# Cumulative decays from split fp32r parts, and rate products on both halves of the rows

## The chip, the cores and the metric

The kernel runs on one core of a Trainium2 chip. The metric is the device time of one execution in microseconds. Three executions of the kernel before took 2044.55 (median), 2040.88 and 2045.95 us. All data is fp32; nothing is computed on the host but the layout of the inputs.

## The reference

The reference is a stack of two transformer blocks on 256 latent and 256 context tokens with 1024 features: a hybrid block (an RWKV mixer beside differential attention), a state-space block, and a second model with three attention branches. The change lies in the RWKV mixer's preparation. Per direction d, with the projections `wd`, `ad`, `k` of the tokens:

```
wlog  = -softplus(-(w0[d] + tanh(wd) @ w_up[d])) - 0.5
decay = exp(-exp(wlog))
a     = sigmoid(a0[d] + ad @ a_up[d])          # the rate
kmod  = k * (1.0 + (a - 1.0) * k_a)
# scan:  s = s * w_t + (s @ -kk_t) b_t + v_t k_t ;  y_t = s @ r_t
```

The scan multiplies a state by a decay at each of 256 steps, forward and backward. The kernel works on chunks of 64 tokens instead of single steps, for which it needs the decays accumulated within each chunk. Since exp(wlog) is exp(-0.5) times sigmoid of `w0 + tanh(wd) @ w_up`, and sigmoid(x) is half of tanh(x/2) + 1, the accumulated log decay is a constant times a running sum of tanh(x/2) + 1 over the chunk's tokens.

## The kernel before, in words

The kernel is a sequence of stages. Each stage is written as Python generators ("streams") that yield a declared cost; `weave` takes the next step from the stream that is least far along. A planner then orders each engine's instructions in advance, by priority and by its own estimate of when operands are ready, and puts in the semaphores; at run time each engine goes through its list in order. Tiles come from pools with a fixed number of buffers per tag, and buffers of a tag are handed out in program order. A stage's pools reuse the memory of the stage before, so its first tiles wait until the last reader of the old ones is done.

The stage of the change is in `hybrid` (L672), between about 46 and 216 us. It has two streams:

- `dense` (L745): 17 projections of 512 columns (256 context, 256 latent tokens). Each is 24 fp32r matmuls (`projs`, L447): weights and activations are split into a rounded high part and a low part (`whi`, `wlo`, `hhi`, `hlo`), and three of the four products are kept. The first projection gives `wdad`: rows 0 to 63 are `wd`, rows 64 to 127 are `ad`. Then come k, r, v for the four pairs of heads p, the gate, and q, k, v of the first attention head.
- `preps` (L766): `rwkv_prep` for p = 0 to 3. It runs with a priority 1000 ahead of the dense stream.

`rwkv_prep(p)` (L1120) first makes the rate: for d = 0, 1 one fp32 product of 64 contraction rows and 512 columns (L1130), tanh (L1132), and `kmod` on VectorE (L1134, L1135). Then come the unit keys (L1145 to L1152), v reversed and transposed (L1159 to L1167) and the bonus (L1172 to L1177). Then, for each direction: `pw`, the product for the decay (L1182, four token blocks), tanh (L1185), plus one (L1186), and for each half s (context, latent) the running sums within chunks, as a product of `w` with a 128x256 matrix of zeros and ones, `tri0` or `tri1` (L1193): its first 128 columns give the inclusive sum, the others the exclusive one. Two exponentials (L1197, L1198) and four VectorE products (L1211 to L1214) give `ar` and `bk`; `bk` is transposed (L1218), copied to SBUF (L1220), and all three are stored to DRAM by GpSimd's DMA queue (`bkd`, `ard`, `btd`, L1221 to L1223). Products on PSUM bank tag `w` take their banks in program order, so the second half's L1193 stands behind the first half's L1218. The tag `mm` has two banks.

A full fp32 product appears in the trace as two matmul instructions, an fp32r product as one. fp32r rounds its operands; a matrix of zeros and ones is exact in it.

After the stage, `rwkv_units` (L930) reads the stored tiles back, beside `diff_attention` (L810) and the modulation products `adas` (L454, matmuls L473, loads `raw<-adaw`). Matmuls of these streams stand in TensorE's list from 186 us on, as far as their buffers allow; the tiles that they need in the pools `DF` and `U` open when the stage's pools `Q` and `X` are free. Weights are loaded by SyncE's queue into four buffers `raw` (L410), in program order.

Of the kernel before, what the change touches and what calls it, by code (L numbers as in the profile page):

```python
# [7 lines left out]
F32 = mybir.dt.float32  # L8
# [294 lines left out]
class Kern:  # L303
# [368 lines left out]
    def hybrid(self):  # L672
# [17 lines left out]
        nc.scalar.dma_start(wup, A['wup'])  # L690
        aup = self.tl(Q, [128, 2, 512], 'aup')
        nc.scalar.dma_start(aup[64:128], A['aup'])
        omm = self.tl(Q, [128, 14], 'omm')
# [11 lines left out]
        nc.vector.tensor_scalar(hrk, self.V('r_k'), 0.5, None, op0=MUL)  # L705
        self.load_consts(5, Q)

        def shifted(b, out):
# [19 lines left out]
        sig = self.sig = self.tl(R, [128, 512], 'sig')  # L728
        wdad = self.tl(Q, [128, 512], 'wdad')
        wt = self.tl(Q, [65, 512], 'wt')  # L730
        t4 = lambda n: [self.tl(Q, [128, 512], n, bufs=4) for _ in range(4)]
# [13 lines left out]
        def dense():  # L745
            yield from shifted(0, wdad)
            nc.scalar.activation(wt[0:64], wdad[0:64], AF.Tanh)
            nc.gpsimd.memset(wt[64:65], 1.0)
            for hf in range(2):
# [16 lines left out]
        def preps():  # L766
            for hf in range(2):
                yield from await_(main, lambda: (hf, 0) in ready)
                yield from unit_keys(hf)
                yield from await_(main, lambda: (hf, 2) in ready)  # L770
                for j in range(2):
                    p = 2 * hf + j
                    yield from self.rwkv_prep(p, ks[p], rr[p], vv[p], yk[hf][:, 8 * j:8 * j + 8], wdad, wt, wup, aup,
                                              ha0, hka, oka, hrk, Q, X)

# [343 lines left out]

    def rwkv_prep(self, p, k, r, v, yk, wdad, wt, wup, aup, ha0, hka, oka, hrk, Q, X):  # L1120

# [4 lines left out]
        nc.vector.tensor_scalar(kok, k, oka[:, p:p + 1], None, op0=MUL)  # L1126
        kms, ts = [], []
        for d in range(2):
            ps = self.PSt('w')
            nc.tensor.matmul(ps, aup[64:128, d, 128 * p:128 * p + 128], wdad[64:128], start=True, stop=True)  # L1130
            t = self.tl(X, [128, 512], 'x1', bufs=2)
            nc.scalar.activation(t, ps, AF.Tanh, scale=0.5, bias=ha0[:, d, p:p + 1])  # L1132
            km = self.tl(Q, [128, 512], 'km', bufs=2)
            nc.vector.tensor_tensor(km, t, k, MUL)  # L1134
            nc.vector.scalar_tensor_tensor(km, km, hka[:, p:p + 1], kok, op0=MUL, op1=ADD)  # L1135
            kms.append(km)
            ts.append(t)
            yield 1.5
# [40 lines left out]
        for d in range(2):  # L1179
            pw = self.PSt('w')  # L1180
            for tt in range(4):
                nc.tensor.matmul(pw[:, 128 * tt:128 * tt + 128], wt[:, 128 * tt:128 * tt + 128],  # L1182
                                 wup[:, d, 128 * p:128 * p + 128], start=True, stop=True)
            w = self.tl(Q, [128, 512], 'w', bufs=1)
            nc.scalar.activation(w, pw, AF.Tanh, scale=0.5)  # L1185
            nc.vector.tensor_scalar(w, w, 1.0, None, op0=ADD)  # L1186
            wh = w.rearrange("p (a b) -> p a b", a=4)
            yield 2.0
            for s in range(2):
                pg = self.PSt('w').rearrange("p (t k c) -> p t k c", t=2, k=2)  # L1190
                for dt in range(2):
                    for i, x in enumerate((wh,)):
                        nc.tensor.matmul(pg[:, dt], x[:, 2 * s + (dt if d == 0 else 1 - dt)], self.C(f'tri{d}'),  # L1193
                                         start=True, stop=True)
                eP = self.tl(X, [128, 2, 2, 128], 'eP', bufs=2)
# [1078 lines left out]
```

## Time and profile before

| | |
|---|---|
| median of three executions | 2044.55 us |
| profiled execution, its own time | 2040.4 us |
| its span | 2038.6 us |
| TensorE busy | 1938.1 us, 95% of the span |
| VectorE busy | 1446.8 us, 71% |
| ScalarE busy | 964.4 us, 47% |
| GpSimd busy | 149.9 us, 7% |
| mean granted TensorE clock | 0.978 of full speed |

Engines are named PE (TensorE matmul), PEld (its weight loads, which overlap), DVE (VectorE), ACT (ScalarE), POOL (GpSimd) and SP (SyncE). L1193 is line 1193 of the kernel. A row such as `168.70 1.13 PE L1193 MATMUL psw<-cst,w ... x4` is four instructions, the first starting at 168.70 us; output left of the arrow, operands right. A matmul's length in the timeline includes its way through the array (some 0.17 us here), so that neighbours overlap; the chain of waits shows what each added. In brackets stands idle time of the engine ahead of the row and what ended it. A granted clock of 1.00 is TensorE's level of 2.4 GHz, 0.50 that of 1.2 GHz.

### The profile page before, as it was taken

What the parts mean: (1) busy time and instruction counts of PE and PEld (TensorE: products, weight loads), DVE (VectorE), ACT (ScalarE), POOL (GpSimd) and SP (SyncE); (2) the same over time, 40 slices, a digit from 0 to 9 for tenths busy, and PEclk for the clock granted to TensorE, in tenths of its full rate; (3) what the DMA queues carried; (4) which work ended last, traced back from release to release, by engine and by line L of the source; (5) the groups of instructions that cost most, each with busy time, mean ns of one, the idle gap of its engine ahead of it and who ended that gap; (6) DMA issues with size and microseconds to landing.
All of it is one profiled execution on the core that took longest, in us unless ns stands there. A gap on an engine that the chain in (4) does not pass through costs nothing.

```text
span 2038.6 us, 37380 instructions
## 1 busy us (share of the span) xinstructions
PE 1938.1 (95%) x14898; PEld 1648.5 (81%) x14898; DVE 1446.8 (71%) x3044; ACT 964.4 (47%) x1770; POOL 149.9 (7%) x273
## 2 busy tenths in 40 slices
PE   6999799969899999998999999999999999999999
PEld 4776456747698899986778878899986888899999
DVE  4675596696699854437988887666678666667984
ACT  3454233322552434434566665566655445456663
POOL 0022401201031200000000003000000000000000
PEclk8999898989899999999999999999999999999999
DMA  7355843413287853322223325466644323345664
GB/s 274 125 175 203 251 155 120 143 42 124 81 271 243 289 169 93 94 88 71 92 64 86 101 73 158 147 186 185 180 148 153 125 93 115 113 147 173 191 190 150
DMA packets 87021, 299.82 MB, mean 147 GB/s; under 512 B 11213, under 2 KB 14685, under 8 KB 86846
## 3 DMA queue, kind: packets, MB, share of 16 engines
q1 hardware_dynamic: 62064, 221.29, 34.1%
q0 software_dynamic: 20736, 69.64, 10.5%
q10 hardware_dynamic: 4046, 6.49, 1.0%
q8 instruction: 117, 1.92, 0.4%
q14 instruction: 58, 0.48, 0.1%
HBM read 281.63 MB, written 18.90 MB: 147 GB/s over the span
## 4 chain that ended last, share of the span: by engine, by line
PE 79%; DVE 8%; DMA 5%; issue 5%; ACT 2%; POOL 1%; POOLq 0%; SPq 0%; DVEq 0%; ACTq 0%
PE psmm L447 23%; PE psmm L426 11%; PE psmm L429 11%; PE psmm L427 11%; DMA ar<-adat 2%; PE psmm L1635 2%; PE psy L1698 2%; PE psw L524 1%; PE psw L1703 1%; DVE wlo L419 1%; PE psa L429 1%; PE psa L426 1%; PE psa L427 1%; PE pso L2054 1%; PE psya L972 1%
## 5 line engine op out<-in xcount | busy, mean ns | idle before, releaser
L418 ACT ACTIVATE whi<-raw 128x1024 fp32r<-128x1024 f32 x374 | 394.4, 1055 | 482.1 <-PE psmm L427 242.2
L419 DVE TENSOR_TENSOR wlo<-raw,whi 128x1024 fp32r<-128x1024 f32 x374 | 453.5, 1213 | 59.4 <-ACT whi L418 39.1
L447 PE MATMUL psmm<-hhi,whi 128*128 128x256 f32 (+1 forms) x1040 | 337.4, 346 | 6.5 <-ACT whi L418 2.1
L447 PE MATMUL psmm<-hlo,whi 128*128 128x256 f32 (+1 forms) x1040 | 330.9, 339 | 2.1 <-DVE hlo L665 1.5
L426 PE MATMUL psmm<-hhi,whi 128*128 128x258 f32 (+1 forms) x944 | 231.1, 283 | 0.3 <-ACT whi L418 0.3
L427 PE MATMUL psmm<-hlo,whi 128*128 128x258 f32 (+1 forms) x944 | 230.8, 282 | 0.0
L447 PEld LDWEIGHTS psmm<-hhi,whi 128*128 128x128 f32 x1040 | 199.8, 192 | 38.1 <-issue 12.2
L447 PEld LDWEIGHTS psmm<-hlo,whi 128*128 128x128 f32 x1040 | 199.7, 192 | 28.7 <-DVE hlo L663 4.8
L447 PE MATMUL psmm<-hhi,wlo 128*128 128x256 f32 (+1 forms) x1040 | 213.5, 336 | 0.2 <-DVE wlo L419 0.2
L426 PEld LDWEIGHTS psmm<-hhi,whi 128*128 128x128 f32 x944 | 178.7, 189 | 2.7 <-issue 1.4
L427 PEld LDWEIGHTS psmm<-hlo,whi 128*128 128x128 f32 x944 | 179.2, 190 | 0.7 <-issue 0.6
L447 PEld LDWEIGHTS psmm<-hhi,wlo 128*128 128x128 f32 x1040 | 157.4, 189 | 25.1 <-issue 9.1
L426 PE MATMUL psmm<-hi,whi 128*128 128x512 f32 (+1 forms) x512 | 164.0, 340 | 5.3 <-ACT hi L668 5.3
L427 PE MATMUL psmm<-lo,whi 128*128 128x512 f32 (+1 forms) x512 | 161.8, 336 | 0.0
L429 PE MATMUL psmm<-hhi,wlo 128*128 128x258 f32 (+1 forms) x944 | 132.0, 282 | 0.0
L429 PEld LDWEIGHTS psmm<-hhi,wlo 128*128 128x128 f32 x944 | 121.0, 190 | 0.0
L426 PEld LDWEIGHTS psmm<-hi,whi 128*128 128x128 f32 x512 | 96.4, 189 | 19.1 <-ACT hi L668 7.0
L511 DVE SCALAR_TENSOR_TENSOR aj<-ar,cb 128x1024 f32<-128x1024 f32 x80 | 97.8, 1222 | 13.2 <-DMA ar<-adat 10.2
L427 PEld LDWEIGHTS psmm<-lo,whi 128*128 128x128 f32 x512 | 96.3, 189 | 10.3 <-DVE lo L669 0.5
L429 PE MATMUL psmm<-hi,wlo 128*128 128x512 f32 (+1 forms) x512 | 100.0, 338 | 0.0
L1370 ACT ACTIVATE r<-r,s 128x256 f32<-128x256 f32 x96 | 48.9, 510 | 87.8 <-DVE r L1369 87.5
L429 PEld LDWEIGHTS psmm<-hi,wlo 128*128 128x128 f32 x512 | 81.6, 190 | 10.4
(607 smaller groups left out, 3649.0 us busy)
## 6 DMA issues: line engine op xcount, KB each, us to landing
raw<-w SPq DMA_DIRECT2D x128, 512.0 KB, 4.1
ar<-adat POOLq DMA_DIRECT2D x56, 512.0 KB, 4.9
raw<-win SPq DMA_DIRECT2D x55, 512.0 KB, 3.5
raw<-ssdin SPq DMA_DIRECT2D x49, 512.0 KB, 3.6
raw<-hyin SPq DMA_DIRECT2D x26, 512.0 KB, 4.1
raw<-adaw SPq DMA_DIRECT2D x24, 512.0 KB, 5.2
raw<-wg SPq DMA_DIRECT2D x22, 512.0 KB, 3.6
raw<-wu SPq DMA_DIRECT2D x22, 512.0 KB, 3.6
```

Of the source, the lines that this page charges most:

```text
L418: nc.scalar.activation(hi[:, :n], raw, AF.Copy)
L419: nc.vector.tensor_tensor(lo[:, :n], raw, hi[:, :n].bitcast(F32), SUB)
L426: nc.tensor.matmul(ps, whi[:, k], act.hi[k][:, n0:n1], start=start and i == 0, stop=False)
L427: nc.tensor.matmul(ps, whi[:, k], act.lo[k][:, n0:n1], start=False, stop=False)
L429: nc.tensor.matmul(ps, wlo[:, k], act.hi[k][:, n0:n1], start=False, stop=stop and i == len(ks) - 1)
L447: nc.tensor.matmul(ps, w[:, k], a[k][:, n0:n1], start=i == 0, stop=i == len(runs) - 1)
L511: nc.vector.scalar_tensor_tensor(junk, raw, 1.0, cb[j], op0=MUL, op1=MUL, accum_out=self.mod[l][:, b, j:j + 1])
L524: self.nc.tensor.matmul(out[32 * g:32 * g + 32, 128 * b:128 * b + 128], self.C('two' if heads else 'one'), sq, start=start, stop=stop, ski ...
L972: nc.tensor.matmul(pss[h][:, q], bk[r, q], ar[r, q], start=True, stop=True)
L1370: nc.scalar.activation(r[:, s], r[:, s], AF.Relu, bias=sh)
L1635: nc.tensor.matmul(ps, w[:, k0 + k], a[k], start=start and i == 0, stop=stop and i == len(runs) - 1, skip_group_check=True)
L1698: nc.tensor.matmul(o, w[:, q], m[:, q], start=d == 0 and n == 2 and q < 2 and k == 0, stop=k == 1 and d == 1 and n == 3, skip_group_check= ...
```

## The change

The running sums become fp32r products. After the tanh, ScalarE writes tanh + 1 rounded to fp32r (`wh`, high part), VectorE writes what the rounding left (`wl`, low part: w + 1 - high), and each running sum is two fp32r products that accumulate, high and low, with fp32r copies of the triangles made once at the start of the stage. VectorE's plus one is gone.

The rate's products of both directions are made together at the start of `rwkv_prep`. The rate weights of direction 0 lie on rows 0 to 63 and of direction 1 on rows 64 to 127; `ad` is copied by two DMAs from `wdad` to both halves of a new tile `wad`. Each direction's 512 columns are two products of 256, and the directions alternate. They stay fp32.

```diff
--- before.py
+++ after.py
@@ -688,8 +688,10 @@
 
         wup = self.tl(Q, [65, 2, 512], 'wup')
         nc.scalar.dma_start(wup, A['wup'])
-        aup = self.tl(Q, [128, 2, 512], 'aup')
-        nc.scalar.dma_start(aup[64:128], A['aup'])
+
+        aup = self.tl(Q, [128, 512], 'aup')
+        for d in range(2):
+            nc.scalar.dma_start(aup[64 * d:64 * d + 64], A['aup'][:, d])
         omm = self.tl(Q, [128, 14], 'omm')
         hm = self.tl(Q, [128, 14], 'hm')
         nc.vector.tensor_scalar(omm, self.V('mu'), -1.0, 1.0, op0=MUL, op1=ADD)
@@ -704,6 +706,9 @@
         nc.vector.tensor_scalar(oka, self.V('k_a'), -0.5, 1.0, op0=MUL, op1=ADD)
         nc.vector.tensor_scalar(hrk, self.V('r_k'), 0.5, None, op0=MUL)
         self.load_consts(5, Q)
+        tri = [self.tl(Q, [128, 256], f'tri{d}', F32R) for d in range(2)]
+        for d in range(2):
+            nc.vector.tensor_copy(tri[d], self.C(f'tri{d}'))
 
         def shifted(b, out):
             po = []
@@ -727,6 +732,7 @@
         self.R, self.DR = R, DR
         sig = self.sig = self.tl(R, [128, 512], 'sig')
         wdad = self.tl(Q, [128, 512], 'wdad')
+        wad = self.tl(Q, [128, 512], 'wad')
         wt = self.tl(Q, [65, 512], 'wt')
         t4 = lambda n: [self.tl(Q, [128, 512], n, bufs=4) for _ in range(4)]
         ks, rr, vv, yk = t4('k'), t4('r'), t4('v'), []
@@ -745,6 +751,8 @@
         def dense():
             yield from shifted(0, wdad)
             nc.scalar.activation(wt[0:64], wdad[0:64], AF.Tanh)
+            nc.scalar.dma_start(wad[64:128], wdad[64:128])
+            nc.scalar.dma_start(wad[0:64], wdad[64:128])
             nc.gpsimd.memset(wt[64:65], 1.0)
             for hf in range(2):
                 for n, x in enumerate((ks, rr, vv)):
@@ -770,8 +778,8 @@
                 yield from await_(main, lambda: (hf, 2) in ready)
                 for j in range(2):
                     p = 2 * hf + j
-                    yield from self.rwkv_prep(p, ks[p], rr[p], vv[p], yk[hf][:, 8 * j:8 * j + 8], wdad, wt, wup, aup,
-                                              ha0, hka, oka, hrk, Q, X)
+                    yield from self.rwkv_prep(p, ks[p], rr[p], vv[p], yk[hf][:, 8 * j:8 * j + 8], wad, wt, wup, aup,
+                                              ha0, hka, oka, hrk, tri, Q, X)
 
         qkv0 = []
         self.banks(**self.PS_PREP)
@@ -1117,7 +1125,7 @@
                 nc.scalar.activation(lt[d][G4[2 * d], ms, 32:64], pt[G4[2 * d]], AF.Copy)
             yield 3.0
 
-    def rwkv_prep(self, p, k, r, v, yk, wdad, wt, wup, aup, ha0, hka, oka, hrk, Q, X):
+    def rwkv_prep(self, p, k, r, v, yk, wad, wt, wup, aup, ha0, hka, oka, hrk, tri, Q, X):
 
         nc = self.nc
         ident = self.C('ident')
@@ -1125,11 +1133,16 @@
         kok = self.tl(X, [128, 512], 'x2', bufs=1)
         nc.vector.tensor_scalar(kok, k, oka[:, p:p + 1], None, op0=MUL)
         kms, ts = [], []
+
+        pas = [self.PSt('w') for _ in range(2)]
+        for i in range(2):
+            for d in range(2):
+                r2 = slice(64 * d, 64 * d + 64)
+                nc.tensor.matmul(pas[d][:, 256 * i:256 * i + 256], aup[r2, 128 * p:128 * p + 128],
+                                 wad[r2, 256 * i:256 * i + 256], start=True, stop=True)
         for d in range(2):
-            ps = self.PSt('w')
-            nc.tensor.matmul(ps, aup[64:128, d, 128 * p:128 * p + 128], wdad[64:128], start=True, stop=True)
             t = self.tl(X, [128, 512], 'x1', bufs=2)
-            nc.scalar.activation(t, ps, AF.Tanh, scale=0.5, bias=ha0[:, d, p:p + 1])
+            nc.scalar.activation(t, pas[d], AF.Tanh, scale=0.5, bias=ha0[:, d, p:p + 1])
             km = self.tl(Q, [128, 512], 'km', bufs=2)
             nc.vector.tensor_tensor(km, t, k, MUL)
             nc.vector.scalar_tensor_tensor(km, km, hka[:, p:p + 1], kok, op0=MUL, op1=ADD)
@@ -1181,17 +1194,20 @@
             for tt in range(4):
                 nc.tensor.matmul(pw[:, 128 * tt:128 * tt + 128], wt[:, 128 * tt:128 * tt + 128],
                                  wup[:, d, 128 * p:128 * p + 128], start=True, stop=True)
+
             w = self.tl(Q, [128, 512], 'w', bufs=1)
             nc.scalar.activation(w, pw, AF.Tanh, scale=0.5)
-            nc.vector.tensor_scalar(w, w, 1.0, None, op0=ADD)
-            wh = w.rearrange("p (a b) -> p a b", a=4)
+            wh = [self.tl(Q, [128, 4, 128], f'w{i}', F32R, bufs=1) for i in 'hl']
+            whf, wlf = (t.rearrange("p a b -> p (a b)") for t in wh)
+            nc.scalar.activation(whf, w, AF.Copy, bias=1.0)
+            nc.vector.scalar_tensor_tensor(wlf, w, 1.0, whf.bitcast(F32), op0=ADD, op1=SUB)
             yield 2.0
             for s in range(2):
                 pg = self.PSt('w').rearrange("p (t k c) -> p t k c", t=2, k=2)
                 for dt in range(2):
-                    for i, x in enumerate((wh,)):
-                        nc.tensor.matmul(pg[:, dt], x[:, 2 * s + (dt if d == 0 else 1 - dt)], self.C(f'tri{d}'),
-                                         start=True, stop=True)
+                    for i, x in enumerate(wh):
+                        nc.tensor.matmul(pg[:, dt], x[:, 2 * s + (dt if d == 0 else 1 - dt)], tri[d],
+                                         start=i == 0, stop=i == 1)
                 eP = self.tl(X, [128, 2, 2, 128], 'eP', bufs=2)
                 eN = self.tl(X, [128, 2, 128], 'eN', bufs=2)
                 nc.scalar.activation(eP, pg, AF.Exp, scale=-0.5 * DEC)
```

## Rows read from the trace of the kernel before

**Rows 1.** Busy us by stretch: PE, PEld, DVE, ACT, POOL; granted clock, DMA share.
```profile
160.00:180.00 20.00, 19.90 (x99) 14.83 (x98) 10.98 (x29) 10.28 (x20) 6.47 (x12) 1.00 0.58 210
```

**Rows 2.** Timeline, all engines, one direction of p = 2: start, length, work.
```profile
166.50 1.06 PE L1182 MATMUL psw<-wup,wt 65*128 65x128 f32 x8
...
167.59 0.60 ACT L1185 ACTIVATE w<-psw 128x512 f32<-128x512 f32 x1 [0.25 <-PE psw L1182]
...
168.22 0.43 DVE L1186 TENSOR_SCALAR w<-w 128x512 f32<-128x512 f32 x1 [1.17 <-ACT w L1185]
...
168.70 1.13 PE L1193 MATMUL psw<-cst,w 128*128 128x256 f32 x4
...
169.93 0.60 ACT L1197 ACTIVATE eP<-psw 128x512 f32<-128x512 f32 x1 [1.74 <-PE psw L1193]
...
171.65 0.42 DVE L1214 TENSOR_TENSOR bk<-km,eN 128x256 f32<-128x256 f32 x1
...
172.21 0.63 PE L1218 MATMUL psw<-cst,bk 128*128 128x128 f32 x4
...
172.67 1.03 PE L1193 MATMUL psw<-cst,w 128*128 128x256 f32 x4
172.92 0.60 ACT L1220 ACTIVATE bt<-psw 128x512 f32<-128x512 f32 x1 [2.12 <-issue]
...
173.79 0.60 ACT L1197 ACTIVATE eP<-psw 128x512 f32<-128x512 f32 x1 [0.27 <-PE psw L1193]
...
176.08 0.63 PE L1218 MATMUL psw<-cst,bk 128*128 128x128 f32 x4
```

**Rows 3.** Timeline of TensorE, end of the stage.
```profile
182.24 2.02 PE L447 MATMUL psmm<-hhi,wlo 128*128 128x512 f32 x8
...
203.80 1.92 PE L473 MATMUL psmm<-raw,scc 128*32 128x512 f32 x14
```

**Rows 4.** Chain that ended last, at the stage's end: start, length, what.
```profile
207.85 7.53 DMA btd<-bt
```

**Rows 5.** Line L1223, all 16 stores of `btd`, issue to landing.
```profile
DMA to landing us min/median/max: 2.3/3.5/7.7
```

**Rows 6.** Timeline of SyncE's DMA issues at the stage's end.
```profile
204.93 0.33 SPq L410 DMA_DIRECT2D raw<-hyin  x1
205.74 6.05 SPq L410 DMA_DIRECT2D raw<-adaw  x4
```

**Rows 7.** Chain that ended last, the stage's middle.
```profile
69.95 1.91 PE psw L1130 x4
...
94.33 0.86 PE psw L1193 x4
```

**Rows 8.** Timeline of TensorE late in the kernel, fp32r, 256 columns.
```profile
1759.15 0.28 PE L426 MATMUL psmm<-ohi,whi 128*128 128x256 f32 x1
1759.26 0.28 PE L427 MATMUL psmm<-olo,whi 128*128 128x256 f32 x1
```

**Rows 9.** Chain that ended last, next stage, alternating row halves.
```profile
222.18 1.09 PE psya L972 x16
```

**Rows 10.** Groups by shape, 46 to 216 us: busy us, mean ns, idle before.
```profile
L1135 DVE SCALAR_TENSOR_TENSOR km<-km,hka,x 128x512 f32<-128x512 f32 x8 | 5.9, 747 | 0.0
```

**Rows 11.** Timeline of ScalarE, after a tanh of p = 2.
```profile
157.43 0.71 ACT L1177 ACTIVATE bon<-bon,vec 128x512 f32<-128x512 f32 x1
```

**Rows 12.** Timeline, engines mixed, start of the stage.
```profile
54.65 0.69 DVE L715 TENSOR_TENSOR sm<-pp 128x512 f32<-128x512 f32 x1 [3.12 <-ACT pp L713]
...
55.66 1.22 DVE L419 TENSOR_TENSOR wlo<-raw,whi 128x1024 fp32r<-128x1024 f32 x1
...
57.57 0.63 ACT L747 ACTIVATE wt<-wdad 64x512 f32<-64x512 f32 x1 [0.16 <-DVE wdad L718]
```

**Rows 13.** Busy time by stretch, where the granted clock falls.
```profile
434.00:438.00 4.00, 1.15 (x8) 0.72 (x6) 3.38 (x16) 0.00 (x0) 0.00 (x0) 1.00 0.00 0
438.00:442.00 4.00, 2.40 (x8) 1.92 (x8) 3.90 (x13) 0.00 (x0) 0.00 (x0) 0.53 0.00 0
```

## The prediction

> **What bounds the kernel now.** I read the page, the windows, the chain of waits, and then the timeline across engines in the stretch that the change touches, 60 to 216 us. There TensorE is busy for 19.90 of 20 us at full clock [rows 1], which looks like a stage bound by TensorE. Two streams share it. The "dense" stream (17 projections, fp32r, 128x512) fills TensorE. The "preps" stream runs `rwkv_prep` for p = 0 to 3, one after another, ahead of the dense stream wherever its instructions are ready. The question is which of the two ends the stage.
>
> The timeline of one direction of p = 2 answers it [rows 2]: decay products (L1182), tanh 167.59, add 168.22, triangle products 168.70, exp 169.93, four DVE products to 172.07, transposes 172.21, second triangle products 172.67, exp 173.79, four more DVE products, transposes 176.08. Each step starts 0.05 to 0.2 us after the one that it needs: the add ends at 168.65 and the products start at 168.70; the last `bk` product ends at 172.07 and the transposes start at 172.21. So TensorE is not late for this chain; dense matmuls only fill the holes. The chain is bound by latency over four engines. It outlives the dense stream, whose last eight matmuls start at 182.24 and end at 184.26 [rows 3], while the last `btd` store of p = 3 is issued at 207.85 [rows 4].
>
> Then comes a stall: that store takes 7.53 us to land [rows 4], and the next stage's tiles reuse the memory it reads. The median of the 16 such stores is 3.5 us, the shortest 2.3 [rows 5]. The late one shares the DMA engines with a `hyin` load issued at 204.93 and four `adaw` loads from 205.74 on [rows 6], 512 KB each.
>
> **The change part by part.** The profiled execution took 2040.4 us around a span of 2038.6; the median of the three runs is 2044.55, 4.15 more. I work in differences against the profiled execution and apply them to the median.
>
> *Triangle products.* 16 groups (4 p, 2 directions, 2 halves). A group is now two fp32 products, four matmul instructions, 0.86 us [rows 7]. It becomes four fp32r products of 256 columns; consecutive fp32r matmuls of that shape start 0.11 us apart with new weights [rows 8], taken as 0.115: 0.46 us. TensorE saves 0.40 x 16 = 6.4 us, 12 x 0.40 = 4.8 of it before the dense stream ends.
>
> *Rate products.* Per p, four instructions of 64 rows take 1.91 us one after the other [rows 7]. After, eight instructions of 256 columns, directions alternating between the two halves of the rows. The nearest row is L972, which alternates row halves the same way: 16 instructions of 128 columns in 1.09 us [rows 9]. At the triangle products' pace (0.86 / 4 = 0.215 per 256 columns) those would take 1.72 one by one, so the ratio is 0.63. Eight of 256 columns: 8 x 0.215 x 0.63 = 1.08, saving 0.83 per p, 3.3 in all. Bounds: no overlap, 2.1 us (0.2 lost per p); perfect overlap, 0.86 (1.05 gained). I take 0.83.
>
> So TensorE loses 9.7 us of work, 4.8 + 3.3 = 8.1 of it before 184.26. Since the dense stream is its fill, the dense stream ends near 176. That is off the path.
>
> *What the path gets.* From tanh to the first exp it takes 169.93 - 167.59 = 2.34 us [rows 2]. After: tanh 0.60 and 0.04 of gap; the new copy on ScalarE, priced by the tanh of the same size, 0.60; hop 0.05; the new DVE subtraction at the fp32 row of its form, 0.747 [rows 10]; hop 0.05; three fp32r products (the first can run while the low part is made), 0.345; then from the products' end to exp, 169.93 - (168.70 + 0.86) = 0.37. Sum 2.80, or 0.46 more, and for 8 directions +3.7. No row shows this copy. Its near row is a ScalarE pass of the same 128x512, hence 0.60; the far ends are nothing, if it were hidden as its neighbours off the chain are, and 1.22, the DVE pass over 128x1024 [rows 12], and they go into the range. In the first direction the bonus activation follows the tanh at 157.43 [rows 11]; it is emitted earlier, so it will stand between tanh and copy: 0.6 for p = 0 to 2 (p = 3 has it ahead of the tanh), +1.8.
>
> In the second half of a direction 0.40 less of products precedes exp, but exp also waits for the `bt` copy ahead of it: 172.92 + 0.49 = 173.41 against 173.79 [rows 2], so 0.38 is the most; I count it in 5 of 8, -1.9. The rate products give their first direction 0.1 earlier, -0.4; the second direction's tanh is 0.8 earlier, but DVE works without a gap behind it. Sum on the chain: 3.7 + 1.8 - 1.9 - 0.4 = +3.2. The last store is issued near 211.
>
> *What comes back.* The loads that crowd the last store follow the dense stream: dense end 184.26, then one group of modulation products, a projection, a second group (its last matmuls from 203.80), which frees the buffers for the load at 204.93 [rows 3, 6]. That is 20.7 us after the dense end. With the dense end at 176 the same loads start near 197, and, at the 10.5 us that they took (204.93 to 215.38), have landed near 207.5, before the last store. That store should then land in about 2.8 us instead of 7.53: -4.7. No further load can follow them early: only two `mm` banks exist, and both stay held until the next stage's tiles open.
>
> *Set at nothing.* Two SBUF copies `wdad` to `wad` by DMA: the tanh beside them starts at 57.57 [rows 12] and the first reader at 69.95 [rows 7]; a store of like size lands in 2.3 to 7.7 us [rows 5], so 4 us of cover remain; ScalarE is not needed by the path for the two issues. Two 128x256 DVE copies of the triangles fit DVE's 3.12 us of idle time before 54.65 [rows 12]; if DVE took them before the constants land, TensorE would lose up to 3 us there. The `aup` load in two parts waits for nothing new. Extra DVE work (8 x 0.32) is on the chain already.
>
> Sum: +3.2 - 4.7 = **-1.5 us**, 2038.9 for the profiled execution, 2043 for the median.
>
> **A rule weighed.** TensorE's granted clock falls when its work thins out: after a stretch with 1.15 of 4 us busy it is 0.53 in the next one, near 0.5, the 1.2 GHz level [rows 13]. The Trainium skill, TensorE: Matmul & The Clock Gate, Part 1, states that throttled is the default and activity releases it. By that rule, taking work off TensorE can cost time in what stays. This speaks against the change; it is rival C.
>
> **The rivals.**
> A. TensorE's throughput does bound the stage: the 8.1 us saved pass to the end, 2036.5. For it: 19.90 of 20 us busy [rows 1]. Against: the hops of 0.05 to 0.2 us [rows 2]. With the shorter landing too, 2032.
> B. Slower: the split chain grows and nothing comes back. Copy and subtraction each join an in-order queue in which dense passes of up to 1.22 us run [rows 12]; at half a microsecond of queueing for each of 8 directions the chain gains 3.2 + 4 = 7.2 us. It decides if the last store is issued more than 6 us later than 207.85 and still takes over 7 us: 2051.7. For it: the bonus pass that slips in at 157.43 [rows 11]. Against: ScalarE and DVE have idle time in this stretch [rows 1].
> C. The tail runs at 1.2 GHz: from about 195 on TensorE would have only the chain's own work: per direction, which takes 176.08 - 166.50 = 9.6 us now, 0.8 of decay products, two transpose groups of 0.45 (172.21 to 172.67) and two product groups of 0.46 [rows 2], 2.6 us in 10, as thin as the stretch before the fall. On the path of the last direction 0.8 + 0.35 + 0.45 + 0.25 + 0.45 = 2.3 us of it would double: -1.5 + 2.3 = +0.8, 2045.4. Against: at 160 to 180 the clock is full [rows 1], and the fill may last longer than I reckon.
> D. The row halves do not overlap: the dense end moves by 4.8 - 0.8 = 4.0 only, the loads land near 211.5, the store gains about 4 instead of 4.7: 2044.
>
> **How the numbers follow.** A difference of 0.3% (6.1 us) is about what a measurement of this kernel can tell from none. Chances: forecast 0.37 (own range 2038 to 2047, since the order of later instructions may shift by a few us), A 0.27, C 0.16, B 0.15, D 0.05. Faster than 2038.4: most of A and a little of the forecast, 0.29. Slower than 2050.7: most of B and tails of C, 0.17. The rest 0.54. The range reaches to A with the landing gain and to B: 2032 to 2051.
>
> **What would show it.** Right: triangle groups of 0.46 us; rate products near 1.1 us per p; dense end near 176; tanh to exp near 2.8 us; last `btd` store issued at 210 to 212 and landing in about 3 us; next stage starting near 214. Wrong: if the last store is issued near 200, TensorE was the bound (A). If it is later than 214, or lands in over 7 us, B. A granted clock of 0.5 before 209 is C. A difference that arises after 260 us is none of these.

## The result, and the profile after

The changed kernel took 2053.15 us (median of 8 runs) against 2040.74 for the kernel before, measured with it: ratio 1.0056, 95% interval [1.0032, 1.0080]. That is a loss of about half a per cent, small but clear of the interval. A second measurement, on chip 7, gave 1.0028 [1.0008, 1.0048]. The forecast was 2043, a gain of 1.5 us. The profiled execution took 2051.4 us around a span of 2049.6, which is 11.0 more than before.

First the stage by windows; the columns are those of [rows 1].

```profile
160.00:180.00 20.00, 16.85 (x93) 11.17 (x91) 6.88 (x20) 9.75 (x20) 4.82 (x9) 1.00 0.37 129
180.00:200.00 20.00, 15.61 (x86) 10.22 (x86) 12.52 (x24) 8.75 (x15) 4.15 (x9) 1.00 0.73 246
196.00:200.00 4.00, 1.10 (x8) 0.92 (x8) 2.85 (x8) 2.99 (x6) 1.43 (x3) 0.99 0.80 227
200.00:204.00 4.00, 2.56 (x12) 2.53 (x12) 1.38 (x5) 0.72 (x2) 1.79 (x4) 0.50 0.99 399
```

The kernel before, 204 to 208 us:

```profile
204.00:208.00 4.00, 2.74 (x22) 1.06 (x15) 1.51 (x5) 1.43 (x3) 1.76 (x4) 1.00 0.77 207
```

TensorE was busy 19.90 of 20 us between 160 and 180 [rows 1]; now it is 16.85. From 196 on it does 1.10 us of work in 4, and from 200 the granted clock is 0.50 (the 1.2 GHz level). Before, it was 1.00 until 208. The last projection of the dense stream ends at 171.8 instead of 184.26, earlier still than the 176 of the forecast. The products of a triangle group start 0.12 us apart where nothing gets between (167.28, 167.40, 167.52), near the 0.115 of the forecast. So the work did leave TensorE, and the time did not get shorter.

The chain, first direction of p = 2, timeline over all engines (start, length, work). It answers to [rows 2]:

```profile
161.65 0.58 ACT L1199 ACTIVATE w<-psw 128x512 f32<-128x512 f32 x1
162.26 0.63 ACT L1202 ACTIVATE wh<-w 128x512 fp32r<-128x512 f32 x1
162.93 0.69 DVE L1203 SCALAR_TENSOR_TENSOR wl<-w,wh 128x512 fp32r<-128x512 f32 x1 [1.94 <-ACT wh L1202]
...
162.94 0.39 PE L1209 MATMUL psw<-tri,wh 128*128 128x256 f32 x1
...
163.86 0.28 PE L1209 MATMUL psw<-tri,wl 128*128 128x256 f32 x1
...
164.41 0.60 ACT L1213 ACTIVATE eP<-psw 128x512 f32<-128x512 f32 x1 [0.77 <-PE psw L1209]
```

Tanh 161.65, copy 162.26, subtraction 162.93, low product 163.86, exp 164.41: 2.76 us, where 2.80 was forecast. This is the undisturbed case. Now the second direction of the same p:

```profile
171.63 0.60 ACT L1199 ACTIVATE w<-psw 128x512 f32<-128x512 f32 x1 [0.29 <-PE psw L1195]
172.60 0.63 ACT L1202 ACTIVATE wh<-w 128x512 fp32r<-128x512 f32 x1
...
173.26 0.69 DVE L1203 SCALAR_TENSOR_TENSOR wl<-w,wh 128x512 fp32r<-128x512 f32 x1 [3.28 <-ACT wh L1202]
...
173.74 0.38 PE L1209 MATMUL psw<-tri,wh 128*128 128x256 f32 x1
...
174.06 1.07 PE L473 MATMUL psmm<-raw,scc 128*32 128x512 f32 x8
...
175.05 0.39 PE L1209 MATMUL psw<-tri,wl 128*128 128x256 f32 x1
...
175.71 0.60 ACT L1213 ACTIVATE eP<-psw 128x512 f32<-128x512 f32 x1 [2.48 <-PE psw L1209]
```

Here the copy stands 0.97 us behind the tanh instead of 0.61, and between the high and the low product (173.74 and 175.05) TensorE's list holds eight modulation products (L473). Tanh to exp takes 4.08 us. The longest is the first direction of p = 0, here on ScalarE alone:

```profile
90.72 0.60 ACT L1199 ACTIVATE w<-psw 128x512 f32<-128x512 f32 x1 [1.27 <-PE psw L1195]
91.22 0.71 ACT L1190 ACTIVATE bon<-bon,vec 128x512 f32<-128x512 f32 x1
91.83 0.62 ACT L1172 ACTIVATE vr<-v 128x512 f32<-128x512 f32 x1
92.35 0.62 ACT L1173 ACTIVATE vr<-v 128x512 f32<-128x512 f32 x1
92.88 0.62 ACT L1202 ACTIVATE wh<-w 128x512 fp32r<-128x512 f32 x1
...
94.92 0.60 ACT L1213 ACTIVATE eP<-psw 128x512 f32<-128x512 f32 x1
```

The bonus pass and two copies of the reversed v stand ahead of the copy, which starts 2.16 us behind the tanh. Over the eight directions tanh to exp takes 4.20, 2.78, 3.17, 3.06, 2.76, 4.08, 3.26 and 3.08; before it was 2.28 to 2.62, 19.61 in sum. The sum grew by 6.8 us, to 26.39.

A third place, TensorE between p = 0 and p = 1 (timeline, matmuls only):

```profile
112.12 0.70 PE L1141 MATMUL psw<-wad,aup 64*128 64x256 f32 x2
112.75 0.33 PE L1234 MATMUL psw<-cst,bk 128*128 128x128 f32 x1
113.00 0.70 PE L1141 MATMUL psw<-wad,aup 64*128 64x256 f32 x2
...
114.33 0.70 PE L1141 MATMUL psw<-wad,aup 64*128 64x256 f32 x2
114.95 0.33 PE L1234 MATMUL psw<-cst,bk 128*128 128x128 f32 x1
...
115.54 0.70 PE L1141 MATMUL psw<-wad,aup 64*128 64x256 f32 x2
```

The eight rate products are pulled apart by transposes, so they end at 116.2 and not 1.1 us after 112.12; the first tanh waits until 115.06 (113.10 before). Where nothing gets between, the eight take 1.1 us:

```profile
147.14 1.13 PE L1141 MATMUL psw<-wad,aup 64*128 64x256 f32 x8
```

The stage's end, from the timelines of SyncE, GpSimd and ScalarE; it answers to [rows 4, 6]:

```profile
193.93 0.33 SPq L410 DMA_DIRECT2D raw<-hyin  x1
195.25 4.85 SPq L410 DMA_DIRECT2D raw<-adaw  x4
...
215.95 0.54 POOL L1239 DMA_DIRECT2D btd<-bt  x1 [1.32 <-ACT bt L1236]
...
218.70 0.60 ACT L879 ACTIVATE vT<-psw 128x512 f32<-128x512 f32 x1 [2.20 <-DMA btd<-bt]
```

The loads start 11 us earlier, and the last store lands 2.7 us after its issue instead of 7.53 [rows 4]. But it is issued at 215.95, 8.1 later than before. The next stage starts (its first `vT` copy, L871 before and L879 after) at 218.7 instead of 215.5: +3.2.

### The profile page after: what moved, and what is told of

The parts are those of the page before. It is cut to its first block, busy times and chain, and to the rows that moved or that the text cites. A ratio compares the mean times of both kernels' runs of the same rounds, so it can differ in the third digit from the quotient of the medians.

```text
span 2049.6 us, 37428 instructions
## 1 busy us (share of the span) xinstructions
PE 1940.5 (95%) x14914; PEld 1655.4 (81%) x14914; DVE 1449.5 (71%) x3046; ACT 968.4 (47%) x1778; POOL 150.0 (7%) x273
## 3 DMA queue, kind: packets, MB, share of 16 engines
q0 software_dynamic: 20736, 69.64, 10.3%
q8 instruction: 117, 1.92, 0.4%
## 4 chain that ended last, share of the span: by engine, by line
PE 63%; DVE 4%; issue 4%; DMA 2%; ACT 1%; POOL 0%; POOLq 0%; DVEq 0%; ACTq 0%
PE psmm L447 18%; PE psmm L426 10%; PE psmm L427 10%; PE psmm L429 10%; DMA ar<-adat 2%; PE psmm L1651 2%; PE psy L1714 2%; PE psw L1719 1%; PE psw L524 1%; PE psa L429 1%; PE psa L426 1%; PE psa L427 1%; PE pso L2070 1%; DVE aj L511 1%; PE psa L2036 1%
## 5 line engine op out<-in xcount | busy, mean ns | idle before, releaser
L427 PEld LDWEIGHTS psmm<-lo,whi 128*128 128x128 f32 x512 | 96.3, 189 | 10.5 <-DVE lo L669 0.7
L1567 DVE SCALAR_TENSOR_TENSOR cu<-psmm,cw,cu 128x508 f32<-128x508 f32 (+3 forms) x128 | 85.8, 675 | 4.5 <-ACT cu L1564 4.1
```

The lines of the kernel that those rows point to most:

```text
L427: nc.tensor.matmul(ps, whi[:, k], act.lo[k][:, n0:n1], start=False, stop=False)
L1567: nc.vector.scalar_tensor_tensor(u[:, :, a:b], pp[:, :, a + k:b + k], cw[:, j, k + 2:k + 3], u[:, :, a:b], op0=MUL, op1=ADD)
```

## The experiments

Three theories stood against each other. Theory 1: the latency chain of the preps sets the stage's end, and the copy and subtraction lengthen it. Theory 2: TensorE was made too thin; its clock and the changed fill cost the time. Theory 3: order or throughput on TensorE. Ratios are to the kernel before, measured in the same session on the same chip; the runs from the one without the low part on are from chip 14, without the change itself beside them.

**One part alone: split triangles.** The rate products stay as before.

> The kernel before with the split triangle products alone (rate products as before). Theory 1 (latency chain): the copy and the subtraction lie on the chain of the preps, tanh to first exp 2.8 to 4.2 us instead of 2.3 to 2.6, eight times +0.85; last btd store issued near 215, and the time is that of the whole change or 1 to 2 us more, 2051 to 2056 against 2041. Theory 2 (thin TensorE): only the TensorE work taken away matters; here 4.8 us less before the dense end instead of 8.1 or more, so the granted clock of the tail falls later than 200 us and the loss is about half, 2045 to 2048.

Measured 1.0046 [1.0033, 1.0058], as slow as the whole change. Tanh to exp is 2.78 to 4.44 us, the last store is issued at 221.0. The expectation was near 215. The clock fell to 0.5 already near 180, so the run does not refute theory 2 by itself.

**One part alone: rate products.** The triangles stay fp32.

> The kernel before with the rate products on row halves alone (triangle products fp32 as before). Theory 1 (latency chain): tanh to first exp stays at 2.3 to 2.6 us, dense end 3 us earlier (181), last btd store issued 207 to 208.5, its landing a little shorter; 2036 to 2042 against 2041, no loss. Theory 2 (thin TensorE): the fill ends earlier and the granted clock falls to 0.5 before 209, the last store is issued 2 us later; 2043 to 2046. Theory 3 (the copies of the decay and rate inputs and the grouped products disturb the order): p = 0 to p = 1 gets 1.5 to 2 us longer as it did in the changed kernel; 2043 to 2045.

Measured 0.9992 [0.9980, 1.0003]: no loss. Tanh to exp stays at 2.26 to 2.62 us in seven of eight directions. But the p = 0 to p = 1 step lost time as theory 3 said: from the last exp of p = 0 to the first rate tanh of p = 1 it takes 6.5 us (107.95 to 114.42) against 3.7 (109.38 to 113.10). The last store is issued at 212.6, later than the 207 to 208.5 expected. It lands sooner, and the next stage starts at 216.1, where it started before. The split is the part that costs.

**The two kernels once more.**

> The changed kernel once more, to see what repeats in another execution. If the losses behind the stage belong to the program: the granted clock falls to 0.5 near 282 to 288 us during the triangular inversion (4 us lost there), and the last feed-forward part runs at 0.118 us a matmul instead of 0.1135 (4 us lost). If they belong to one execution, one of them or both are gone, and the span differs from 2049.6 by that. Time 2048 to 2056 in either case.

> The kernel before once more, one profile: the spread of the same stretches without any edit. If the stretches behind 220 us belong to the program, the inversion takes 40 us again, the clock stays at 1.0 there, and the last feed-forward part runs at 0.1135 us a matmul. If not, these two vary by some us from one execution to another, and no cause in the change is to be looked for there.

The change is the second measurement above, 1.0028 [1.0008, 1.0048]; the kernel before had one profile (2047.0 us). What I had put down to the program is partly the execution's. Busy time in the last feed-forward part, 1900 to 1960 us, of the kernel before and then of its second profile:

```profile
1900.00:1960.00 60.00, 60.00 (x531) 60.00 (x531) 56.84 (x111) 41.54 (x67) 0.00 (x0) 1.00 0.63 194
```

```profile
1900.00:1960.00 60.00, 60.00 (x512) 60.00 (x511) 54.52 (x106) 39.89 (x64) 0.00 (x0) 1.00 0.61 189
```

The same program at the same granted clock does 531 matmuls in one execution and 512 in the other. The first profile of the change was at 511. Of the fourteen profiles of this document three ran at 531 or 532 (the first of the kernel before, rate products alone, high part only), the others at 511 or 512. So some 4 of the 11 us between the first two profiles are not the change's. The clock moves too. Here are 182 to 190 us of the change, first and second profile, and then 282 to 286 of the same two:

```profile
182.00:190.00 8.00, 7.76 (x44) 6.02 (x42) 6.29 (x10) 2.84 (x5) 1.67 (x4) 1.00 0.98 380
...
282.00:286.00 4.00, 3.90 (x10) 2.42 (x11) 3.19 (x8) 1.19 (x5) 0.00 (x0) 0.50 0.92 332
```

```profile
182.00:190.00 8.00, 6.83 (x29) 5.29 (x30) 4.57 (x10) 3.79 (x7) 1.86 (x4) 0.57 0.98 350
...
282.00:286.00 4.00, 1.92 (x23) 1.39 (x20) 4.00 (x18) 1.53 (x2) 0.00 (x0) 1.00 0.82 288
```

The first execution lost 4.0 us in the triangular inversion at half clock: from its first to its last update of `Xi` it took 40.3 us, against 36.3 in the second and 36.2 and 36.5 in the two profiles of the kernel before. The second kept the clock there, but had lost it at 182 and started the next stage at 223.4. At the end of the next stage (start of the last `x` copy, L1016 before, at 509.8) the two are 9.9 and 10.5 us late.

**A shorter chain, a thinner TensorE.** The low part is left out, so the decays lose their lower bits.

```
-            nc.vector.scalar_tensor_tensor(wlf, w, 1.0, whf.bitcast(F32), op0=ADD, op1=SUB)
...
-                    for i, x in enumerate(wh):
+                    for i, x in enumerate(wh[:1]):
```

> The change without the low part: no subtraction on VectorE and no low product, so the decays lose their lower bits (output not the reference's). TensorE has still less to do (a triangle group of 0.23 us), the chain loses its second added pass. Theory 1 (the latency chain sets the end): tanh to first exp 0.60 + 0.05 + 0.60 + 0.05 + 0.23 + 0.37 = 1.9 us where nothing gets between, against 2.3 to 2.6 before and 2.8 to 4.2 in the change; last btd store at 204 to 208, ratio to before 0.996 to 1.000. Theory 2 (thin TensorE and its clock): the loss is as large as the change's or larger, 1.003 to 1.006.

Measured 0.9974 [0.9955, 0.9993], although TensorE has the least to do of all, and its clock is at 0.5 from 176 to 180 and from 196 on. The last store is issued at 210.0, not at 204 to 208. Timeline, first direction of p = 2:

```profile
158.78 0.58 ACT L1199 ACTIVATE w<-psw 128x512 f32<-128x512 f32 x1
159.38 0.63 ACT L1202 ACTIVATE wh<-w 128x512 fp32r<-128x512 f32 x1
...
160.07 0.50 PE L1208 MATMUL psw<-tri,wh 128*128 128x256 f32 x2
160.61 0.60 ACT L1212 ACTIVATE eP<-psw 128x512 f32<-128x512 f32 x1 [0.59 <-PE psw L1208]
```

1.83 us from tanh to exp here, 19.37 in sum over the eight, against 19.61 before, although the ScalarE copy is still there. Theory 2 has the wrong sign.

**A longer chain, TensorE as before.** Two passes on the path, fp32 products.

```
+            nc.scalar.activation(w2, w, AF.Copy, bias=1.0)
+            nc.vector.scalar_tensor_tensor(w3, w, 1.0, w2, op0=ADD, op1=MAX)
```

> The kernel before with two passes on the decay path as in the change (a copy plus 1 on ScalarE, then a VectorE pass of the subtraction's form, here the maximum of two equal values), but the fp32 triangle products and the rate products as before, so TensorE's work is that of before. Theory 1 (latency chain): tanh to first exp 2.4 + 0.97 = 3.3 us or more, eight times +0.97, last btd store at 215 to 219; ratio 1.003 to 1.005, about the loss of the change. Theory 2 (thin TensorE): TensorE has no less to do, so no loss, 0.999 to 1.001.

Measured 1.0047 [1.0029, 1.0064]: with TensorE's work that of before, the loss is there. Timeline, first direction of p = 2:

```profile
165.72 0.58 ACT L1185 ACTIVATE w<-psw 128x512 f32<-128x512 f32 x1
166.34 0.63 ACT L1188 ACTIVATE wh<-w 128x512 f32<-128x512 f32 x1
167.00 0.69 DVE L1189 SCALAR_TENSOR_TENSOR wl<-w,wh 128x512 f32<-128x512 f32 x1 [1.94 <-ACT wh L1188]
...
168.92 0.60 ACT L1200 ACTIVATE eP<-psw 128x512 f32<-128x512 f32 x1 [1.20 <-PE psw L1196]
```

3.20 us here, 3.19 to 5.16 over the eight. The last store is issued at 225.4, later than the 215 to 219 expected: the passes queue here as well, and the fp32 products stay as long as they were, so that the chain grows by more than in the change (tanh to exp 31.3 in sum). The clock of the tail falls too, to 0.50 from 204 on, so the kernel ahead of this one and the one behind it tell the clock from the chain, and this one does not.

**The same split without the ScalarE pass.**

```
-            nc.scalar.activation(whf, w, AF.Copy, bias=1.0)
+            nc.vector.tensor_scalar(whf, w, 1.0, None, op0=ADD)
```

> The change with the high part made by VectorE (add 1, written as fp32r, the add's place and size as before) instead of a ScalarE copy. TensorE's work is that of the change. Theory 1 (latency chain): no ScalarE pass and none of its neighbours (bonus, vr copies) between tanh and exp; 0.60 + 0.05 + 0.43 + 0.05 + 0.75 + 0.05 + 0.12 + 0.37 = 2.4 us from tanh to first exp against 2.8 to 4.2; last btd store 4 to 6 us earlier than in the change, ratio 0.999 to 1.002. Theory 2 (thin TensorE): no difference to the change, 1.003 to 1.006.

Measured 1.0007 [0.9992, 1.0021]: no loss is left that this can tell from none. The interval lies below the first one of the change and overlaps the second. Timeline, p = 2:

```profile
157.62 0.60 ACT L1199 ACTIVATE w<-psw 128x512 f32<-128x512 f32 x1 [2.05 <-PE psw L1195]
158.12 0.59 ACT L770 ACTIVATE o<-psmm 128x512 f32<-128x512 f32 x1
158.26 0.43 DVE L1202 TENSOR_SCALAR wh<-w 128x512 fp32r<-128x512 f32 x1
158.60 0.72 ACT L1190 ACTIVATE bon<-bon,vec 128x512 f32<-128x512 f32 x1
```

A dense eviction (L770) and the bonus pass still run behind the tanh on ScalarE, but nothing of the chain waits for them now. Tanh to exp is 2.48 to 3.12 us, 22.1 in sum against 26.4 in the change and 19.6 before. The last store is issued at 213.5, only 2.4 us earlier than in the first profile of the change (4 to 6 expected). The clock is at 0.5 from 197 on, in the change from 200 on, and the next stage starts at 216.0.

**TensorE filled up again, two ways.** Once with 48 superfluous products at the end of the dense stream, once with twelve ahead of the transposes of `bk` in each half direction of p = 2 and 3. One line of each:

```
+                nc.tensor.matmul(fill, act.hi[i % KT][:, 0:128], act.hi[i % KT][:, 0:512], start=True, stop=True)
...
+                        nc.tensor.matmul(pb[:, 256 * (i % 2):256 * (i % 2) + 256], wh[i % 2][:, i % 4], tri[d],
```

> The change with 48 superfluous fp32r products of 512 columns (0.23 us each, 11 us in all, results unused) at the end of the dense stream, so that the fill of TensorE lasts about as long as before the change; the preps and their order are those of the change. Theory 1 (chain and, in its tail, the clock): the granted clock is 1.00 from 180 to at least 205 us, tanh to first exp stays at 2.8 to 4.2 us, last btd store at 211 to 214 where it was 216 and 221; ratio 1.001 to 1.004. Theory 2 (thin TensorE is the whole cause): as before, ratio 0.999 to 1.001, last btd store at 207 to 209. Theory 3 (TensorE's throughput bounds the stage): 11 us more work, 1.006 or more.

> The change with twelve superfluous fp32r products of 256 columns (0.11 us each, results overwritten) ahead of the second transposes of each half direction of p = 2 and 3, so that TensorE stays busy in the tail. Theory 1 (latency chain): the granted clock stays at 1.00 between 180 and 218 us, the last direction gets back what it lost at 0.5 (L1195 x8 at 1.06 instead of 1.92 us), last btd store at 211 to 214 instead of 216 to 221; the rest of the loss stays, ratio 1.001 to 1.003. Theory 2 (thin TensorE is the whole cause): ratio 0.998 to 1.000. Theory 3 (TensorE's order bounds the tail): the fillers delay the products behind them and it gets slower than the change, 1.005 or more.

The first measured 1.0031 [1.0012, 1.0049]: giving TensorE its work back does not give the time back. Tanh to exp is 2.77 to 4.20 as in the change. The clock held to 194 and was mixed after that, not at 1.00 to 205 as expected, and the last store is issued at 215.1. Since the loads now follow a longer fill, it also lands late again: the next stage starts at 221.7.

The second measured 1.0001 [0.9985, 1.0017], for a reason that no theory named. The fillers delay the first half's transposes: in TensorE's list the second half's products (165.50) now stand ahead of them (166.57), so both halves' exps stand side by side: exp to exp 1.7 us in p = 2 and 3 instead of 3.4 to 4.3. The clock stayed at 1.00 to 220, the last store was issued at 205.0. The next stage starts at 207.8, 7.7 earlier than before, at full clock. At the last `x` copy, 509.8 before, this execution is 8.5 late. The next stage gave back 16 us.

**The order by itself.** That hint made three kernels: the loop over the two halves is cut in two, so that the products, exps and VectorE products of both come ahead of the transposes and stores of both. The edit, shortened:

```
                 yield 2.5
+                halves.append((bk, ar))
+            for s, (bk, ar) in enumerate(halves):
                 ps = self.PSt('w').rearrange("p (s c) -> p s c", s=4)
```

> The kernel before with the loop over the two halves of a direction cut in two: triangle products, exps and VectorE products of both halves first, then transposes, copies and stores of both (three buffers for bk and ar instead of two). No arithmetic is changed. Theory 1 (latency chain): exp to exp falls from 3.8 to 1.7 to 2.5 us, as it did where the fillers made the program order so; a direction takes 8 to 9 us instead of 10.4, last btd store at 192 to 202 instead of 208. Whether the time follows: if the next stage can start on it, ratio 0.993 to 0.998; if its loads and its thin stretches set the pace there, as in the kernel with the fillers (8 us earlier at the end of this stage, 8 us later at 540), 0.999 to 1.003. Theory 3 (TensorE's throughput): last btd store moves by less than 2 us.

> The same loop cut in two, with the rate products on row halves (fp32 triangles). Theory 1: last btd store as in the kernel with the loop cut alone or up to 3 us earlier, since TensorE has 3.3 us less to do where it is fuller now; ratio 0.992 to 1.002. If the p = 0 to p = 1 step loses its 2 to 2.5 us again (rate products pulled apart by transposes), the two are equal.

> The loop cut in two, with the whole change and the high part made by VectorE (two buffers for bk and ar, for space). Theory 1: tanh to first exp 2.4 to 3.1 us, exp to exp 1.5 to 2.5; last btd store at 194 to 204; with TensorE 9.7 us lighter the clock of the tail falls to 0.5 near 180 to 190, which costs 2 to 5 us; ratio 0.995 to 1.002. If two buffers make the next direction wait for stores to land, exp to the next tanh grows by 2 us or more.

Measured 0.9995 [0.9977, 1.0014], 0.9986 [0.9968, 1.0004] and 0.9993 [0.9975, 1.0011]. The last store is issued at 193.6, 194.5 and 198.7 instead of 207.8. In the first of them no arithmetic is changed: the stage was bound by latency and order, and TensorE's throughput allowed 14 us less. Exp to exp fell to 0.76 to 0.87 us where the rows stand apart, below the 1.5 to 2.5 expected. In the second the p = 0 to p = 1 step lost some 2 us again, as its expectation said. The half clock of the tail expected in the third did not come: it is 1.00 to 204. Yet none of the gain arrives in the time. Of the second of them, windows in the next stage (the columns of [rows 1]):

```profile
200.00:215.00 15.00, 11.58 (x60) 7.68 (x60) 9.23 (x23) 2.85 (x7) 10.18 (x14) 0.89 0.97 297
215.00:230.00 15.00, 10.79 (x75) 7.60 (x76) 5.81 (x13) 2.39 (x7) 8.14 (x11) 0.89 0.90 222
...
280.00:300.00 20.00, 17.90 (x124) 11.04 (x124) 15.55 (x31) 3.95 (x9) 0.00 (x0) 0.74 0.40 135
```

The DMA engines are at 0.90 to 0.97 for the first 30 us (before, at 0.82 and 0.90 in the 30 us from 215 on), and the granted clock is 0.74 between 280 and 300, where it was 1.00 before. The lead melts on the way: 15.6 us where the next stage starts, 10.5 at the first update of `Xi`, 5.7 at its last (the inversion takes 41.1 us instead of 36.2), 2.2 at the last `x` copy. What bounds that stretch is not settled: loads, the diff attention beside it and the clock all fit.

The whole set, in us of the profiled executions (last store issued; start of the next stage; start of its last `x` copy), with the ratio:

```
before                        207.8   215.5   509.8
before, second profile        208.5   216.0   512.3
change                        215.9   218.7   519.7   1.0056
change, second profile        221.0   223.4   520.3   1.0028
triangles alone               221.0   224.0   526.6   1.0046
rate products alone           212.6   216.1   510.2   0.9992
high part only                210.0   213.8   507.0   0.9974
two passes, fp32              225.4   228.3   524.1   1.0047
split on VectorE              213.5   216.0   514.3   1.0007
fill at the dense end         215.1   221.7   516.6   1.0031
fillers in the chain          205.0   207.8   518.3   1.0001
loop cut, before              193.6   199.2   508.8   0.9995
loop cut, rate products       194.5   199.9   507.6   0.9986
loop cut, split on VectorE    198.7   202.0   511.3   0.9993
```

Every kernel whose next stage starts at 216.1 or earlier measured 0.9974 to 1.0007, every one that starts it at 218.7 or later 1.0028 to 1.0056. That is what links the stage's end to the time. Within each group the order does not follow the start, and the last `x` copy, seen in one execution each, does not order the ratios either (518.3 goes with 1.0001). One that starts early gains nothing: starts at 199 to 208 end at 507.6 to 518.3.

## Why the prediction was wrong

It had the stage right and the sum wrong. The step that failed is the sum on the chain, "3.7 + 1.8 - 1.9 - 0.4 = +3.2": it was +8.1. The steps of the chain add up to it as follows, in us against the kernel before, first profiles and then second ones (in brackets p = 0 to 3 or the three changes of p, first profiles):

```
first rate tanh of p = 0                                -1.4    +0.2
tanh to exp, eight directions                           +6.8    +6.7
exp to exp of the two halves, eight                     -0.7    +0.1
last exp of a p to the rate tanh of the next            +1.1    +3.0   (+1.8, -0.8, +0.1)
rate tanh to the first decay tanh                       +0.7    +1.1   (-0.8, -1.5, +2.9, 0.0)
second exp to the tanh of the other direction           +1.2    +1.1   (0.0, +0.2, 0.0, +1.0)
last exp to the last store                              +0.4    +0.4
last store                                              +8.1   +12.5
```

*Tanh to exp.* Forecast 5.5 us, measured 6.8 in one execution and 6.7 in the other. The term is right where nothing gets between, 2.76 against 2.80. Eight times 2.80 would be 22.4; the 4.0 us that are left of 26.39 are queueing, where I had counted 1.8 for the bonus pass. Of these, 2.8 stand between tanh and copy on ScalarE: 1.55 in the first direction of p = 0, behind the bonus pass and two copies of v, and 0.36 to 0.50 in three others; in p = 2 the bonus pass does not stand there at all. Rival B's mechanism is this, and its price, half a microsecond a direction, is what was measured; its other half, that nothing comes back, did not come true. What I had costed as a copy and a subtraction are two more places in in-order queues, and a split product is two entries of TensorE's list, between which eight products of another stream slipped.

*Second halves.* Forecast -1.9, measured -0.7. The products got shorter, but exp waits for the `bt` copy, as [rows 2] showed (173.41 against 173.79); I had taken nearly all of that slack. In the change the second exp stands directly behind that copy in all directions but the last, as here in p = 2:

```profile
167.36 0.60 ACT L1236 ACTIVATE bt<-psw 128x512 f32<-128x512 f32 x1 [2.07 <-PE psw L1234]
167.86 0.59 ACT L1213 ACTIVATE eP<-psw 128x512 f32<-128x512 f32 x1
```

*Rate products.* Forecast -0.4. Their size was right (1.1 us against 1.08, so rival D is refuted), their place between p = 0 and p = 1 was not. The first direction's tanh needs the first and the third pair of products, and transposes of 128 rows got between them: the third pair starts at 114.33, the tanh at 115.06. From the last exp of p = 0 (109.57) that is 5.5 us instead of 3.7, +1.8. The Trainium skill, TensorEngine Tiling (Array Packing), Key Properties, states that a change of tiling mode drains TensorE. The trace agrees: with one transpose between them it is 0.88 us from pair to pair (112.12 to 113.00), against 0.28 in the consecutive eight (1.13 / 4), and the transpose itself explains only 0.11 of the difference (115.12, 115.23 and 115.34 are the starts of three that follow each other). I had not weighed that rule.

*Steps that I did not have.* From the rate tanh to the decay tanh p = 2 took 13.3 us instead of 10.4, in both executions. On VectorE wide passes, of the dense stream and of the rate itself, now stand between the small steps of the norm: the last one of those (L563) starts at 147.84 before and 153.32 after. That the earlier dense stream is the reason is argued, not shown, and p = 0 and p = 1 got 0.8 and 1.5 us back in the same step. Still, "off the path" was wrong for the dense stream: it shares VectorE's queue with the chain.

*The tail's clock.* Rival C came true: 0.50 from 200 on. The last direction took 12.5 us from store to store (203.48 to 215.95) against 10.3 before (197.57 to 207.85). Two kernels with the same fall, the high part only and the split on VectorE, show that it does not make a kernel slow by itself. It has a part in the +1.2 and the +0.4 above: the eight decay products of the last direction take 1.92 us instead of 1.06.

*What comes back.* Right: the loads started at 193.93 (forecast 197), and the last store landed in 2.7 us (forecast 2.8). With the chain at +8.1 the 4.8 us were not enough.

*Rival A.* Refuted by the runs with the loop cut: TensorE could end 14 us earlier.

*Behind the stage.* "A difference that arises after 260 us is none of these" was a mistake of principle. Of the 11.0 us between the two profiles 3.2 stand at the stage's end and 9.9 at the last `x` copy; 4.1 more arise in the last feed-forward part, which the same program shows at either pace, and 3 are gained back elsewhere on the way. Between 218 and 520 the change lost 6.7 us in one execution (9.9 - 3.2), 4.1 of it in the inversion, and 2.6 in the other (10.5 - 7.9). Where the clock falls in that stage differs from one execution to the next, so how much of it belongs to the change stays open. The time is explained in its sign and by the group of late starts, not to the microsecond.

## What to carry to other kernels

A product split into high and low parts is cheaper on the matmul engine and, where it adds passes to a chain, longer in latency: on a chain across engines, count each new instruction as a place in an in-order queue, and ask what stands ahead of it. Here either of two steps did away with the loss: leaving out VectorE's subtraction, or making the high part on VectorE in the place of the add, out of ScalarE's queue, which keeps the low part. Look for an order that overlaps the halves before you shorten a product. Before taking a gain at a stage's end for a gain in time, find out what the next stage waits for; here starts that were 13 to 16 us earlier came to nothing.

## What the hardware showed that I had not expected

The last feed-forward part runs at 531 or at 512 matmuls per 60 us in two executions of the same kernel, TensorE busy throughout and the granted clock 1.00 in both: 4 us that no edit made. And the half clock came at 182 us in one execution of the changed kernel and not in the other, after stretches that were equally thin: TensorE was busy for 2.01 and 2.08 of the 4 us from 178 to 182, at a granted clock of 1.00 in both, and from 182 to 184 the clock was 0.57 in the one and 1.00 in the other. A single pair of profiles can't tell such a difference from an edit's; a second profile of each kernel did.
